# Feed-forward gate and up products turned round: weights stationary, both token halves moving, from the fifth width block on

## The chip, the core and the metric

The kernel runs on one core of a Trainium2 chip. A time is the device time of one execution in microseconds (us); the kernel before was timed three times. TensorE (PE in the profile) multiplies: it holds a 128x128 *stationary* operand, loaded by its own instruction (PEld), and streams a *moving* operand of up to 512 columns through it into a PSUM bank. VectorE (DVE) and ScalarE (ACT) read PSUM and on-chip memory; SyncE (SP) issues the transfers. Each engine works through its own queue in order.

## The reference

Two layers over 256 tokens of width 1024. In each, four token mixers and their gates are summed, projected and added to x, and then comes the part that is changed, a feed-forward block with inner width 2816:

```python
h = rmsnorm(x, g_pre_ffn[l])
f = (jax.nn.silu(h @ w_ffn_gate[l]) * (h @ w_ffn_up[l])) @ w_ffn_down[l]
x = x + rmsnorm(f, g_post_ffn[l])
```

## The kernel before

**Products.** Every operand of a large product is split into two float32r parts, high and low, and a product is made of three passes (`mac`): high x high, low x high, high x low. Tokens lie in two halves of 128. For most products a half's activations (`hh` high, `hl` low, transposed to 128 rows of width by 128 tokens) are stationary, and a weight tile moves.

**Weights.** They come in pieces of 128 x 1024 in the order of use (`PLAN`). `stage` loads a piece into one of four `st` buffers; `convert` (L253, ScalarE) writes its high part; `settle` (L272, VectorE) writes the low part by a subtraction. Both parts lie in `u` slots, of which there are 24, shared with what the attention keeps. `pump` runs ahead of the use as long as slots are free and fewer than six unused pieces lie ready; `tick`, called after every *unit* of the main stream (one piece for one half), calls it, and also moves on the work that runs beside (`spawn`, with a delay counted in ticks). The order of all queues follows from the order in which the program emits; nothing is rearranged later.

**Feed-forward.** The inner width is taken in six blocks (512, 256, 512, 512, 512, 512). For each block and half, gate and up products go into a PSUM bank of 128 tokens x 512. `gate_evict` multiplies with the token's 1/rms (`rf[h]`, one number per partition, since tokens lie on partitions) under the sigmoid, `g_act` multiplies with up, then TensorE transposes the result in blocks of 128x128 (`tp`, L403), and ScalarE and VectorE split it into two `s2k` tiles, the stationary operands of the down products, which run one width block behind. The last two width blocks' down products come at the end of the layer, half 0 first, with the norm (`bank_done`, `g_turn`, `final`).

**The step ahead of it.** The output projection does half 0 first, then half 1. `g_turn` for a half sums squares (ScalarE), takes 1/sqrt by three Newton steps (`rsqrt`, nine small VectorE operations), updates x, transposes it (TensorE), writes `hh` (ScalarE, L483) and `hl` (VectorE, L486), and then by the squares of the new x computes `rf[h]`. Its parts come at fixed tick distances. The first width block starts with seven units of half 0 (`lead_order`), while half 1 is still being turned; before half 1's first unit everything of its `g_turn` that isn't emitted yet is emitted (`finish`).

Of the kernel before, what the change touches and what calls it, by code (L numbers as in the profile page):

```python
# [26 lines left out]
FFW = [512, 256, 512, 512, 512, 512]  # L27
FFO = [0, 512, 768, 1280, 1792, 2304]
# [20 lines left out]
# column groups of w_in: (name, [column ranges])  # L49
# [8 lines left out]
# per-layer tables of small operands (one row per partition): SM large, SG gains and the like  # L58
# [46 lines left out]
def uses(key):  # L105
    """How many units of the program read the piece."""
    return 4 if key[1] in ("uq", "ukv") or key[1:3] == ("fd", len(FFW) - 1) else 2


def kxn(w, k0, nk, cols):  # L110
    """Rows k0*128.. of w (nk blocks of 128) and the columns, as [128, nk * ncols]."""
    parts = [w[k0 * P:(k0 + nk) * P, a:b] for a, b in cols]
    m = np.concatenate(parts, axis=1) if len(parts) > 1 else parts[0]
    n = m.shape[1]
    return m.reshape(nk, P, n).transpose(1, 0, 2).reshape(P, nk * n)


def q_cols(hd):
    """The columns of a head of w_uq: the rope part as it is and with its halves exchanged, beside the rest."""
    o = 96 * hd  # L120
    rp = [(o + 64, o + 96), (o + 80, o + 96), (o + 64, o + 80)]
    return [(o, o + 64)] + rp if hd % 2 == 0 else rp + [(o, o + 64)]


def host_piece(inp, key):
# [16 lines left out]
    if g in ("fg", "fu"):  # L142
        w = FFW[key[2]]
        nk = PIECE // w
        return kxn(inp["w_ffn_gate" if g == "fg" else "w_ffn_up"][l], nk * key[3], nk, [(FFO[key[2]], FFO[key[2]] + w)])
    if g == "fd":
        return kxn(inp["w_ffn_down"][l], FFO[key[2]] // P + key[3], 1, [(0, 1024)])
# [15 lines left out]
def host_const(inp):  # L163
    """Tables that follow from the shapes alone (rope cos and sin, 1/count of the first tokens) and the gains."""
# [22 lines left out]
def trunk(ctx: ExitStack, tc, x, xT, wall, small, const, qtab, gpost, out):  # L187
# [30 lines left out]
    def U(shape, dt=F32):  # L218
        """One of the 4 KB slots that the weights share with what the attention keeps."""
        return T(shape, "u4", NU, dt, wp)  # L220

    def keep(shape):
# [3 lines left out]
        return U(shape)  # L226

# [15 lines left out]
    def cuts(i, w):  # L243
        """The first pieces come in two parts, so that the first products start early."""
# [22 lines left out]
    def settle(keep=0, between=()):  # L267
        """Emit the low parts still owed, all but the last few."""
# [8 lines left out]
    def pump(n=1, between=()):  # L277
        """Load and split up to n pieces, while there is room for them."""
# [24 lines left out]
    def mac(out_, a, aw, w, ws, start, stop):  # L303
        """out += a^T w in three passes; a, w are pairs (hi, lo) of float32r tiles."""
# [58 lines left out]
    def g_rsqrt(res, m, n, m2=None):  # L363
        """res gets 1 / sqrt(m (+ m2) + EPS) for [P, n], by Newton's iteration in steps."""
# [51 lines left out]
    def unit(l, name, i, h, st_, out_, width, nk=2):  # L416
        """Products of half h with piece i of a group (nk blocks of rows), then a step of what runs beside."""
# [6 lines left out]
    def pairs(npc):  # L424
        """The halves in turn, two pieces each."""
# [3 lines left out]
    def lead_order(n):  # L429
        """Units of two halves, half 0 first at the start of a phase."""  # L430
# [3 lines left out]
    def trail_order(n):  # L434
        """Units of two halves, half 0 done early at the end of a phase."""
# [23 lines left out]
    def bank_done(po, n, gp, tn):  # L459
        """The part of a norm that needs one bank: its sum of squares and its product with the gains."""  # L460
# [7 lines left out]
    def g_turn(tn, h, g, hT, rs):  # L468
        """x += rmsnorm * gains for half h, then (x * g)^T in hT[h] and rstd of x in rs[h]."""
# [7 lines left out]
        hh, hl = hT_tiles(h)  # L477
# [19 lines left out]
    def final_start(tn):  # L497
        """EPS and the first bank's part of the mean square, for the last half."""
# [72 lines left out]

    for l in range(NL):
# [7 lines left out]
        def rope(h, dst, src, nh):  # L580
            """dst, src: [P, nh, 32]"""
# [77 lines left out]
        def g_bank(h, b, hp, po):  # L659
            """Scores, softmax and values of the hp heads from b * hp on, for the queries of half h."""  # L660
# [68 lines left out]
        st = {}  # L729

        def g_misc():
# [18 lines left out]
            # convolution  # L750
# [14 lines left out]
            # pooling  # L765
# [29 lines left out]
            # spatial gating  # L795
# [100 lines left out]
        # sigmoid(v) = (1 + tanh(v / 2)) / 2; the last half is taken with the sum  # L896
# [62 lines left out]
        rf = [None, None]  # L959
        hF = [None, None]  # L960
        gturn = [None, None]
        po = [[acc(), acc()] for _ in range(2)]
        tns = [[], []]
        for h, u in trail_order(8):
# [5 lines left out]
            if u == 7:  # L970
                gturn[h] = spawn(g_turn(tns[h], h, sg["gpf"], hF, rf), 0)
# [4 lines left out]
        pd = [None, None]  # L976
        act = {}
        nff = len(FFW)

        def gate_evict(h, pg_, w):  # L980
            sg_ = tok()
            nc.scalar.activation(sg_[:, :w], pg_[:, :w], AF.Sigmoid, scale=rf[h])  # L982
            a = tok()
            nc.vector.scalar_tensor_tensor(a[:, :w], pg_[:, :w], rf[h], sg_[:, :w], op0=ALU.mult, op1=ALU.mult)  # L984
            return a

        def g_act(c, h, pu_, a, w):
            nc.vector.scalar_tensor_tensor(a[:, :w], pu_[:, :w], rf[h], a[:, :w], op0=ALU.mult, op1=ALU.mult)
            yield AY
            t = tp()  # L990
            transposes(t, [a[:, i * P:(i + 1) * P] for i in range(w // P)])
            ah = T([P, 4, P], "s2k", 10, F32R)
            al = T([P, 4, P], "s2k", 10, F32R)
            split_copy(ah.rearrange("p k t -> p (k t)")[:, :w], al.rearrange("p k t -> p (k t)")[:, :w], t[:, :w])
            act[c, h] = (ah, al)

        def down_units(c, h):
            nk = FFW[c] // P
            if c < nff - 1:
                return [(c, h, [i], [0, 1]) for i in range(nk)]  # L1000
            return [(c, h, [i, i + 1], [n]) for n in range(2) for i in range(0, nk, 2)]

        def down(u):
            c, h, ks, ns = u
            for i in ks:
                pc_ = W((l, "fd", c, i))
                for n in ns:
                    mac(pd[h][n], act[c, h], np.s_[:, i, :], pc_, np.s_[:, n * 512:(n + 1) * 512],
                        start=(c == 0 and i == 0), stop=(c == nff - 1 and i == FFW[c] // P - 1))

        gact = {}
        for c, w in enumerate(FFW):
            nkp = PIECE // w
# [98 lines left out]
```

## Time and profile before

| | |
|---|---|
| median of three runs | 809.22 us (808.39 to 810.48) |
| profiled execution, span from first to last instruction | 808.4 us |
| its own time beside the span | no more than the lowest run, 808.39 us |
| TensorE products busy | 797.1 us, 99% |
| TensorE weight loads busy | 662.2 us, 82% |
| VectorE busy | 535.3 us, 66% |
| ScalarE busy | 426.4 us, 53% |
| mean share of the 16 transfer engines | 54% for the weight queue |

In the rows below, a line of the timeline has the start, the duration, the engine, the line of the code, the operation with what it writes and reads, the shape, and how many like it follow one another; in brackets stands the idle time just before and what ended it. A group row has the count, the busy time, the mean in ns, and the idle time. A row of TensorE ends by a model and overlaps the next one, so what one product costs is the distance between starts.

### The profile page before, as it was taken

The numbers are of one execution on the slowest core, as the hardware profiler recorded it, in microseconds if no ns is written. First come the engines' busy times: TensorE is split into PE (matmuls) and PEld (weight loads), VectorE is DVE, ScalarE is ACT, GpSimd is POOL, SyncE is SP. The second block draws the span as 40 slices with busy tenths as digits, with TensorE's granted clock in tenths as the row PEclk, the third lists the DMA queues.
The fourth block names the chain that finished last, engine by engine and source line by source line (L and its number), as shares of the span: only waits on it lengthen the run. The fifth ranks groups of instructions, "written<-read, shape, count | busy, mean of one in ns | idle before, by whom it ended". The sixth has DMA issues, their size and how long they took to land.

```text
span 808.4 us, 10402 instructions
## 1 busy us (share of the span) xinstructions
PE 797.1 (99%) x3857; PEld 662.2 (82%) x3857; DVE 535.3 (66%) x895; ACT 426.4 (53%) x672; POOL 3.9 (0%) x16
## 2 busy tenths in 40 slices
PE   8999999999999999999999999999999999999996
PEld 7878887888789888888888888878888988888885
DVE  5687976657786456554785788765689754554553
ACT  6768655535655335443575686554466534543441
POOL 0000000000000000000000000000000000000000
PEclk9999999999999999999999999999999999999999
DMA  8776454464574555664555645346464574665531
GB/s 272 280 250 207 160 182 145 147 225 160 185 222 159 194 179 171 206 207 155 199 165 183 220 168 183 131 157 206 164 224 160 183 234 156 186 216 154 174 105 52
DMA packets 42226, 148.08 MB, mean 183 GB/s; under 512 B 4672, under 2 KB 5824, under 8 KB 42176
## 3 DMA queue, kind: packets, MB, share of 16 engines
q1 hardware_dynamic: 41600, 145.33, 54.0%
q0 software_dynamic: 576, 2.10, 0.7%
q8 instruction: 30, 0.49, 0.3%
q14 instruction: 20, 0.16, 0.1%
HBM read 146.36 MB, written 1.05 MB: 182 GB/s over the span
## 4 chain that ended last, share of the span: by engine, by line
PE 94%; DMA 3%; DVE 1%; ACT 1%; SPq 0%; issue 0%; DVEq 0%; ACTq 0%
PE acc L305 19%; PE acc L307 19%; PE acc L306 19%; PE mm L307 10%; PE mm L305 10%; PE mm L306 10%; PE tp L403 4%; DMA st<-wall 2%; PE mm L667 1%; DMA x<-x 1%; PE acc L695 1%; DVE u L272 0%; ACT junk L393 0%; ACT u L253 0%; SPq L237 0%
## 5 line engine op out<-in xcount | busy, mean ns | idle before, releaser
L272 DVE TENSOR_TENSOR u<-st,u 128x1024 fp32r<-128x1024 f32 (+2 forms) x272 | 320.0, 1207 | 61.6 <-ACT u L253 61.1
L253 ACT ACTIVATE u<-st 128x1024 fp32r<-128x1024 f32 (+2 forms) x272 | 278.2, 1045 | 76.2 <-DMA st<-wall 72.9
L305 PE MATMUL acc<-u,hh 128*128 128x512 f32 (+1 forms) x464 | 185.9, 401 | 0.8 <-ACT hh L540 0.8
L307 PE MATMUL acc<-u,hh 128*128 128x512 f32 (+1 forms) x464 | 181.0, 390 | 1.0 <-DVE u L272 1.0
L306 PE MATMUL acc<-u,hl 128*128 128x512 f32 (+1 forms) x464 | 180.6, 389 | 0.0
L305 PE MATMUL mm<-u,hh 128*128 128x512 f32 (+1 forms) x368 | 137.3, 373 | 0.0
L307 PE MATMUL mm<-u,hh 128*128 128x512 f32 (+1 forms) x368 | 136.6, 371 | 0.5 <-DVE u L272 0.5
L306 PE MATMUL mm<-u,hl 128*128 128x512 f32 (+1 forms) x368 | 136.4, 371 | 0.0
L307 PEld LDWEIGHTS acc<-u,hh 128*128 128x128 f32 x464 | 87.7, 189 | 19.8 <-DVE u L272 2.2
L305 PE MATMUL acc<-u,s2k 128*128 128x512 f32 x256 | 103.5, 404 | 0.0
L305 PEld LDWEIGHTS acc<-u,hh 128*128 128x128 f32 x464 | 87.8, 189 | 17.7 <-ACT hh L540 1.5
L306 PEld LDWEIGHTS acc<-u,hl 128*128 128x128 f32 x464 | 87.8, 189 | 16.0 <-DVE hl L545 0.3
L307 PE MATMUL acc<-u,s2k 128*128 128x512 f32 x256 | 100.4, 392 | 0.0
L306 PE MATMUL acc<-u,s2k 128*128 128x512 f32 x256 | 100.1, 391 | 0.0
L307 PEld LDWEIGHTS mm<-u,hh 128*128 128x128 f32 x368 | 69.3, 188 | 12.8 <-DVE u L272 0.9
L306 PEld LDWEIGHTS mm<-u,hl 128*128 128x128 f32 x368 | 69.4, 188 | 11.8
L305 PEld LDWEIGHTS mm<-u,hh 128*128 128x128 f32 x368 | 69.3, 188 | 11.7
L307 PEld LDWEIGHTS acc<-u,s2k 128*128 128x128 f32 x256 | 48.1, 188 | 11.0
L950 ACT ACTIVATE gate<-acc,rhalf 128x512 f32<-128x512 f32 x32 | 22.1, 690 | 66.1 <-PE acc L307 66.0
L305 PEld LDWEIGHTS acc<-u,s2k 128*128 128x128 f32 x256 | 48.2, 188 | 9.4 <-issue 0.3
L306 PEld LDWEIGHTS acc<-u,s2k 128*128 128x128 f32 x256 | 48.2, 188 | 9.1
L984 DVE SCALAR_TENSOR_TENSOR tok<-mm,ry,tok 128x512 f32<-128x512 f32 (+1 forms) x22 | 15.4, 700 | 58.8 <-ACT tok L982 58.8
(138 smaller groups left out, 568.0 us busy)
## 6 DMA issues: line engine op xcount, KB each, us to landing
st<-wall SPq DMA_DIRECT2D x261, 512.0 KB, 4.4
st<-wall SPq DMA_DIRECT2D x7, 416.0 KB, 4.1
gpost<-gpost POOLq DMA_DIRECT2D x4, 512.0 KB, 3.8
x<-x SPq DMA_DIRECT2D x1, 1024.0 KB, 7.5
small<-small SPq DMA_DIRECT2D x2, 512.0 KB, 4.2
u<-xT SPq DMA_DIRECT2D x3, 256.0 KB, 8.3
st<-wall SPq DMA_DIRECT2D x2, 256.0 KB, 4.4
out<-x SPq DMA_DIRECT2D x2, 256.0 KB, 2.0
```

The source lines that it names most:

```text
L253: nc.scalar.activation(hi[:, a:b], st[:, a:b], AF.Copy)
L272: nc.vector.tensor_tensor(lo[:, a:b], st[:, a:b], hi.bitcast(F32)[:, a:b], op=ALU.subtract)
L305: nc.tensor.matmul(out_, a[0][aw], w[0][ws], start=start, stop=False)
L306: nc.tensor.matmul(out_, a[1][aw], w[0][ws], start=False, stop=False)
L307: nc.tensor.matmul(out_, a[0][aw], w[1][ws], start=False, stop=stop)
L403: nc.tensor.transpose(dst[:, i * P:(i + 1) * P], s, ident)
L667: nc.tensor.matmul(s3[:, i, :], qT[hd // 4][:, hd % 4, h * P:(h + 1) * P], kT[hd % 2][:, hd // 2, 0:kend], start=True, stop=True)
L695: nc.tensor.matmul(o, v_sb[kb][:, hd, :], pT[:, j * P:(j + 1) * P], start=(kb == 0), stop=(kb == nkb - 1))
L950: nc.scalar.activation(gt[h], pgt[h], AF.Tanh, scale=rhalf[h])
L984: nc.vector.scalar_tensor_tensor(a[:, :w], pg_[:, :w], rf[h], sg_[:, :w], op0=ALU.mult, op1=ALU.mult)
```

## The change

The first width block (512, blocks 0 to 3 of 128) stays as it was. From the fifth block of 128 on, up to the 22nd, gate and up are computed transposed, in blocks of 128 of the inner width: the weight block is stationary and the tokens move. `hx` holds for each of eight row blocks the high parts of both halves and the low parts of both halves side by side (512 columns), in four of the `u` slots, reserved before the output projection and given back after the last gate_up. Per row block, one product with the high weight moves all 512 columns, and one with the low weight moves the 256 high ones. `total` adds the two parts of the bank and multiplies with `rrow`, the 1/rms of the tokens along the free dimension, which `g_rrow` makes by transposing two tiles of copies of `rf`. The result needs no transpose: it is split as it is. Down products run four blocks of 128 behind (`DLAG`), the last eight at the end as before. Pieces of gate and up are now read by one unit each, and `tick` is called in the middle of each product block and again after it.

```diff
-FFW = [512, 256, 512, 512, 512, 512]
-FFO = [0, 512, 768, 1280, 1792, 2304]
+FW = 512
+NB = DFF // P
+B0 = FW // P
+DLAG, DLAST = 4, 8
...
+def down_after(b):
+
+    return [b - DLAG] if b - DLAG < NB - DLAST else []
...
-        for c, w in enumerate(FFW):
-            np_ = 8 * w // PIECE
-            plan += [((l, "fg", c, i), 1024) for i in range(np_)]
-            plan += [((l, "fu", c, i), 1024) for i in range(np_)]
-            if c > 0:
-                plan += [((l, "fd", c - 1, i), 1024) for i in range(FFW[c - 1] // P)]
-        c = len(FFW) - 1
-        plan += [((l, "fd", c, i), 1024) for i in range(FFW[c] // P)]
+        plan += [((l, g, i), 1024) for g in ("fg", "fu") for i in range(8 * FW // PIECE)]
+        for b in range(B0, NB):
+            plan += [((l, "wg", b), 1024), ((l, "wu", b), 1024)]
+            plan += [((l, "fd", i), 1024) for i in down_after(b)]
+        plan += [((l, "fd", i), 1024) for i in range(NB - DLAST, NB)]
...
+        hx = []
+        state["reserve"] += NK // 2
+
+        def hx_parts(h):
+            if not hx:
+                hx[:] = [keep_r([P, 2, 2, SEQ]) for _ in range(NK // 2)]
+            return Part(hx, 0, h), Part(hx, 1, h)
...
-                gturn[h] = spawn(g_turn(tns[h], h, sg["gpf"], hF, rf), 0)
+                gturn[h] = spawn(g_turn(tns[h], h, sg["gpf"], hF, rf, hx_parts), 0)
...
+        rrow = T([P, SEQ], "rrow", 1)
+
+        def g_rrow():
+
+            rb = tok()
+            for h in range(2):
+                nc.vector.tensor_copy(rb[:, h * P:(h + 1) * P], rf[h].to_broadcast([P, P]))
+            yield 1
+            t = tp()
+            transposes(t, [rb[:, h * P:(h + 1) * P] for h in range(2)])
+            nc.scalar.copy(rrow, t[:, :SEQ])
+
+        def block(key):
+
+            pc_ = W((l,) + key)
+            o = mm()
+            for k in range(NK):
+                ws = np.s_[:, k * P:(k + 1) * P]
+                nc.tensor.matmul(o, pc_[0][ws], hx[k // 2][:, k % 2].rearrange("p s t -> p (s t)"),
+                                 start=(k == 0), stop=False)
+                nc.tensor.matmul(o[:, :SEQ], pc_[1][ws], hx[k // 2][:, k % 2, 0, :], start=False, stop=(k == NK - 1))
+                if k == NK // 2 - 1:
+                    tick()
+            return o
+
+        def total(dst, o):
+            nc.scalar.copy(dst, o[:, SEQ:2 * SEQ])
+            nc.vector.tensor_tensor(dst, o[:, 0:SEQ], dst, op=ALU.add)
+            nc.vector.tensor_tensor(dst, dst, rrow, op=ALU.mult)
+
+        def gate_up(b):
+            v, sg_ = tok(), tok()
+            gv, uv = v[:, 0:SEQ], v[:, SEQ:2 * SEQ]
+            total(gv, block(("wg", b)))
+            nc.scalar.activation(sg_[:, :SEQ], gv, AF.Sigmoid)
+            nc.vector.tensor_tensor(gv, gv, sg_[:, :SEQ], op=ALU.mult)
+            tick()
+            total(uv, block(("wu", b)))
+            nc.vector.tensor_tensor(gv, gv, uv, op=ALU.mult)
+            t = T([P, 2, SEQ], "s2k", 10, F32R)
+            split_copy(t[:, 0, :], t[:, 1, :], gv)
+            for h in range(2):
+                act[b, h] = (t[:, 0, h * P:(h + 1) * P], t[:, 1, h * P:(h + 1) * P])
+            tick()
...
+        for h, u in lead_order(8):
+            if u == 0:
+                finish(gturn[h])
+                if h == 1:
+                    rr = spawn(g_rrow(), 1)
...
+        finish(rr)
+        for b in range(B0, NB):
+            gate_up(b)
+            if b == B0:
+                pd = [[acc(), acc()] for _ in range(2)]
+            for i in down_after(b):
+                for h in range(2):
                     if i == 0:
...
+                        finish(gact[h])
+                    down((h, [i], [0, 1]))
                     tick()
...
+        drop(NK // 2)
```

How the queues change is seen at three places. The first is TensorE in the first width block, first layer, between the second and the third unit of half 1. Here `u_418` and `u_428` are weight pieces (`u_421` before), `u_437` and `u_438` are parts of `hx`, and `tok` holds the copies of `rf`. Before:

```order
L306 MATMUL acc_2247<-u_418_1927,hl_470_2165 128x512 [waits DVE_49]
L307 MATMUL acc_2247<-u_419_1928,hh_469_2164 128x512
L305 MATMUL acc_2247<-u_421_1939,hh_469_2164 128x512 [waits Activation_49]
L306 MATMUL acc_2247<-u_421_1939,hl_470_2165 128x512 [waits DVE_49]
L307 MATMUL acc_2247<-u_422_1940,hh_469_2164 128x512
```

Now:

```order
L320 MATMUL acc_2236<-u_419_1928,u_437_2019 128x512
L416 MATMUL tp_2257<-ident_69,tok_2243 128x128 [waits DVE_49] x2
L318 MATMUL acc_2236<-u_428_1985,u_438_2020 128x512 [waits Activation_49]
L319 MATMUL acc_2236<-u_428_1985,u_438_2020 128x512
L320 MATMUL acc_2236<-u_429_1986,u_438_2020 128x512
```

Two transposes that wait for VectorE now stand between the units.

The second place is VectorE while half 1 is turned, same layer: the last `hl`, then `rf` of half 1 (`ms`, `rv`, `ry`, `ra`). Before:

```order
L486 SCALAR_TENSOR_TENSOR hl_470_2165<-tp_2192,cst_74,hh_469_2164 128x128 x3
L272 TENSOR_TENSOR u_474_2183<-st_2125,u_473_2182 128x1024 [waits DMAHW1_49]
L272 TENSOR_TENSOR u_479_2209<-st_2137,u_478_2208 128x1024 [waits DMAHW2_49,Activation_49]
L372 SCALAR_TENSOR_TENSOR rv_2234<-ms_2217 128x1 [waits Activation_49]
L373 TENSOR_SCALAR ry_2235<-rv_2234 128x1 [waits DVE_49]
L374 TENSOR_SCALAR rv_2234<-rv_2234 128x1 [waits DVE_49]
L272 TENSOR_TENSOR u_485_2226<-st_2149,u_484_2225 128x1024 [waits DMAHW3_49,PE_49,Activation_49]
L378 SCALAR_TENSOR_TENSOR ra_2236<-ry_2235,rv_2234 128x1 [waits DVE_49]
```

Now:

```order
L499 SCALAR_TENSOR_TENSOR u_439_2021<-tp_2193,cst_74,u_439_2021 128x128 x2
L285 TENSOR_TENSOR u_475_2184<-st_2128,u_474_2183 128x1024 [waits DMAHW1_49,PE_49]
L385 SCALAR_TENSOR_TENSOR rv_2224<-ms_2213 128x1 [waits Activation_49]
L386 TENSOR_SCALAR ry_2225<-rv_2224 128x1 [waits DVE_49]
L387 TENSOR_SCALAR rv_2224<-rv_2224 128x1 [waits DVE_49]
L391 SCALAR_TENSOR_TENSOR ra_2226<-ry_2225,rv_2224 128x1 [waits DVE_49]
...
L395 SCALAR_TENSOR_TENSOR ry_2225<-ra_2226,ry_2225 128x1 [waits DVE_49]
L1034 COPY tok_2243<-ry_2084 128x128
L1034 COPY tok_2243<-ry_2225 128x128 [waits DVE_49]
```

One weight subtraction instead of two stands ahead of the steps and none among them, and the two copies for `rrow` close them.

The third place is ScalarE in the output projection, where half 0's two banks are squared (`junk`). Before:

```order
L253 ACTIVATE u_418_1927<-st_1882 128x1024 [waits DMAHW1_49,DVE_49]
L253 ACTIVATE u_421_1939<-st_1894 128x1024 [waits DMAHW2_49,DVE_49]
L393 ACTIVATE junk_1950,ms_1948<-acc_1865 128x512 [waits PE_49]
L253 ACTIVATE u_427_1962<-st_1913 128x1024 [waits DMAHW3_49,DVE_49]
L393 ACTIVATE junk_1971,ms_1948<-acc_1866 128x512 [waits PE_49,Activation_49]
```

Now:

```order
L266 ACTIVATE u_418_1927<-st_1882 128x1024 [waits DMAHW1_49,DVE_49]
L406 ACTIVATE junk_1945,ms_1943<-acc_1865 128x512 [waits PE_49]
L406 ACTIVATE junk_1960,ms_1943<-acc_1866 128x512 [waits PE_49,Activation_49]
L266 ACTIVATE u_428_1985<-st_1894 128x1024 [waits DMAHW2_49,DVE_49]
L266 ACTIVATE u_431_1997<-st_1913 128x1024 [waits DMAHW3_49,DVE_49]
```

Two conversions have moved behind the second square.

More of the change, by code (lines that the diff above doesn't have):

```diff
@@ L226, in keep, with keep_r @@
         return U(shape)
+    def keep_r(shape):
+        state["free"] -= 1
+        state["reserve"] -= 1
+        assert state["free"] >= 0 and state["reserve"] >= 0
+        return U(shape, F32R)
     def drop(n):
@@ L985, in gate_evict, with g_act @@
             return a
-        def g_act(c, h, pu_, a, w):
-            nc.vector.scalar_tensor_tensor(a[:, :w], pu_[:, :w], rf[h], a[:, :w], op0=ALU.mult, op1=ALU.mult)
+        def g_act(h, pu_, a):
+            nc.vector.scalar_tensor_tensor(a[:, :FW], pu_, rf[h], a[:, :FW], op0=ALU.mult, op1=ALU.mult)
             yield AY
             t = tp()
-            transposes(t, [a[:, i * P:(i + 1) * P] for i in range(w // P)])
+            transposes(t, [a[:, i * P:(i + 1) * P] for i in range(B0)])
@@ L992, in g_act @@
             ah = T([P, 4, P], "s2k", 10, F32R)
             al = T([P, 4, P], "s2k", 10, F32R)
[L994 to L1001, printed above, removed]
+            split_copy(ah.rearrange("p k t -> p (k t)"), al.rearrange("p k t -> p (k t)"), t)
@@ new lines, in g_act @@
+            for i in range(B0):
+                act[i, h] = (ah[:, i, :], al[:, i, :])
+        rrow = T([P, SEQ], "rrow", 1)
[18 more added lines that the diff above has]
+            return o
@@ L1003, in down, with down_units @@
+        def down_units(h):
+            i = NB - DLAST
+            return [(h, [b], [0, 1]) for b in range(i, NB - 4)] + \
+                   [(h, [b, b + 1], [n]) for n in range(2) for b in range(NB - 4, NB, 2)]
         def down(u):
-            c, h, ks, ns = u
-            for i in ks:
-                pc_ = W((l, "fd", c, i))
+            h, bs, ns = u
+            for b in bs:
+                pc_ = W((l, "fd", b))
                 for n in ns:
-                    mac(pd[h][n], act[c, h], np.s_[:, i, :], pc_, np.s_[:, n * 512:(n + 1) * 512],
-                        start=(c == 0 and i == 0), stop=(c == nff - 1 and i == FFW[c] // P - 1))
@@ new lines, in down @@
+                    mac(pd[h][n], act[b, h], np.s_[:, :], pc_, np.s_[:, n * 512:(n + 1) * 512],
+                        start=(b == 0), stop=(b == NB - 1))
+        gact = [None, None]
+        pb, a = {}, {}
+        for h, u in lead_order(8):
[3 more added lines that the diff above has]
+                    rr = spawn(g_rrow(), 1)
+            g, i = u // 4, u % 4
+            if i == 0:
+                pb[h, g] = mm() if h == 0 else acc()
+            unit(l, (("fg", "fu")[g],), i, h, hF, pb[h, g], FW)
+            if i == 3:
+                if g == 0:
+                    a[h] = gate_evict(h, pb[h, 0])
+                else:
+                    gact[h] = spawn(g_act(h, pb[h, 1], a[h]), 0)
+            tick()
@@ L1053, in trunk @@
         hT, rstd = [None, None], [None, None]
-        us = [down_units(nff - 2, h) + down_units(nff - 1, h) for h in range(2)]
+        us = [down_units(h) for h in range(2)]
         tns = [[], []]
```

74 lines of the change are left out of this document (23 added, 51 removed).

## The prediction

> **What bounds the kernel now.** I read the page first: busy shares, then the chain of waits.
>
> ```profile
> PE 797.1 (99%) x3857; PEld 662.2 (82%) x3857; DVE 535.3 (66%) x895; ACT 426.4 (53%) x672; POOL 3.9 (0%) x16
> PE 94%; DMA 3%; DVE 1%; ACT 1%; SPq 0%; issue 0%; DVEq 0%; ACTq 0%
> ```
>
> TensorE is busy 99% of the span and is 94% of the chain that ended last. So the change is worth what it takes from or adds to TensorE's own row of work, and whatever makes TensorE wait. The span is 808.4 us, equal to the lowest run (808.39) within the rounding, so nothing lies around it; the median of the three runs is 809.22, 0.8 above. I sum against 808.4 and add 0.8 at the end.
>
> A busy TensorE row lasts longer than its share of the queue, so prices come from the spacing of starts in the timeline. First the 512-column products and a group of four transposes, then the products of 256 columns, then the weight loads under them (a group row):
>
> ```profile
> 258.03 0.38 PE L403 MATMUL tp<-ident,tok 128*128 128x128 f32 x2
> 258.48 0.39 PE L306 MATMUL acc<-u,s2k 128*128 128x512 f32 x1
> ...
> 318.10 0.60 PE L403 MATMUL tp<-ident,tok 128*128 128x128 f32 x4
> 318.78 0.40 PE L306 MATMUL acc<-u,s2k 128*128 128x512 f32 x1
> 319.01 0.39 PE L307 MATMUL acc<-u,s2k 128*128 128x512 f32 x1
> 321.07 0.40 PE L307 MATMUL acc<-u,s2k 128*128 128x512 f32 x1
> 327.26 0.39 PE L305 MATMUL mm<-u,hh 128*128 128x512 f32 x1
> 344.50 0.39 PE L306 MATMUL mm<-u,hl 128*128 128x512 f32 x1
> ```
>
> ```profile
> 65.49 0.28 PE L305 MATMUL mm<-s2k,u 128*128 128x256 f32 x1
> 66.76 0.28 PE L307 MATMUL mm<-s2k,u 128*128 128x256 f32 x1
> 244.12 0.28 PE L305 MATMUL mm<-u,hh 128*128 128x256 f32 x1
> 247.60 0.28 PE L307 MATMUL mm<-u,hh 128*128 128x256 f32 x1
> ```
>
> ```profile
> L307 PEld LDWEIGHTS mm<-u,hh 128*128 128x128 f32 x368 | 69.3, 188 | 12.8 <-DVE u L272 0.9
> ```
>
> 512 columns: 76 starts from 327.26 to 344.50 make 0.2268 us each (gate and up), 9 from 319.01 to 321.07 make 0.2289 (down). 256 columns: 29 from 244.12 to 247.60 make 0.120, 11 from 65.49 to 66.76 (weights stationary) make 0.1155. The weight loads take 0.188 each and still the products start every 0.120, so the loads are hidden even at 256 columns.
>
> **Part 1: transposes of the results go.** From 318.10 to 318.78 stand four transposes and one product: 0.68 - 0.229 = 0.45. A pair (258.03 to 258.48) costs 0.45 - 0.229 = 0.22. Per layer four wide blocks lose 8 groups of four, the narrow one 2 pairs: 8 x 0.45 + 2 x 0.22 = 4.05, in two layers **-8.1**. The new rrow adds a pair per layer: **+0.4**.
>
> **Part 2: the products.** For one 128-wide block and one of the 8 row blocks the old wide form spends 1.5 products of 512 columns (six over four blocks): 0.340. The narrow form spends three of 256: 0.360. The new form is one of 512 and one of 256: 0.2268 + 0.120 = 0.347; low end 0.2268 + 0.1155 = 0.342, high end 0.2289 + 0.120 = 0.349. Per layer that is 16 x 2 x 8 = 256 such pairs from wide blocks and 32 from the narrow one. Low: 512 x 0.002 - 64 x 0.018 = 0. High: 512 x 0.009 - 64 x 0.011 = +3.9. I take **+2.0**, the middle: the weights are stationary as in the 0.1155 row, but the moving tile is a u slot held like those of the 0.120 row.
>
> The columns streamed are the same; what grows is the number of weight loads, by 576 - 480 = 96 a layer. [...]
>
> **Part 3: rrow makes TensorE wait.** The two transposes of rrow stand in TensorE's queue after nine units of the first block (seven of half 0, two of half 1), and their input needs rstd of half 1, a chain of ScalarE squares, nine tiny VectorE steps and two copies. Before, that rstd was needed only by gate_evict, on other engines. Rows of the first layer, then of the second, then an undisturbed run of the nine steps, then the nearest row for a broadcast copy:
>
> ```profile
> 218.84 0.39 PE L305 MATMUL mm<-u,hh 128*128 128x512 f32 x1
> 232.01 0.39 PE L305 MATMUL acc<-u,hh 128*128 128x512 f32 x1
> ...
> 230.15 1.12 DVE L486 SCALAR_TENSOR_TENSOR hl<-tp,cst,hh 128x128 fp32r<-128x128 f32 x4
> 231.19 2.35 DVE L272 TENSOR_TENSOR u<-st,u 128x1024 fp32r<-128x1024 f32 x2
> ...
> 232.06 0.18 ACT L393 ACTIVATION_READ_ACCUMULATOR junk<-x 128x1 f32 x1
> ...
> 627.84 0.39 PE L305 MATMUL acc<-u,hh 128*128 128x512 f32 x1
> ...
> 627.01 2.35 DVE L272 TENSOR_TENSOR u<-st,u 128x1024 fp32r<-128x1024 f32 x2
> ...
> 397.35 0.15 DVE L372 SCALAR_TENSOR_TENSOR rv<-ms 128x1 f32<-128x1 f32 x1
> 399.06 0.16 DVE L382 SCALAR_TENSOR_TENSOR ry<-ra,ry 128x1 f32<-128x1 f32 x1
> L602 DVE COPY kr<-kr 128x96 f32<-128x96 f32 x4 | 1.0, 253 | 0.1
> ```
>
> TensorE enters the block at 218.84 and would issue the pair at 232.01. In VectorE's new order one 1024-wide subtraction (not two) stands between the last hl and the nine steps: 231.19 + 1.13 = 232.3. ScalarE's squares are done by 232.24 even in the old order, with a conversion ahead that is now gone. Nine steps: 399.22 - 397.35 = 1.9. Two copies, the second starting behind the first: about 0.5. So rrow's input is there at 234.7, 2.7 us after TensorE asked. Second layer: 627.01 + 1.13 + 1.9 + 0.5 = 630.5 against 627.84, again 2.7. Together **+5.4**. Low end, if the subtraction falls behind the steps: 2 x 1.6 = 3.2; high end, if another stands ahead: 2 x 3.8 = 7.6. Queued behind the waiting pair are the rest of half 1's products, so nothing of it is hidden: TensorE has no slack to give back.
>
> **Part 4: a stall in the first layer goes.** Reserving four slots for hx before the output projection takes weight conversions out of ScalarE's queue there (the order rows above).
>
> ```profile
> 207.39 1.06 ACT L253 ACTIVATE u<-st 128x1024 fp32r<-128x1024 f32 x1 [2.77 <-DMA st<-wall]
> 208.36 0.58 ACT L393 ACTIVATE junk<-acc 128x512 f32<-128x512 f32 x1
> ...
> 211.58 1.42 DVE L474 SCALAR_TENSOR_TENSOR x<-mrg,ry,x 128x512 f32<-128x512 f32 x2
> ...
> 211.13 0.39 PE L307 MATMUL acc<-u,hh 128*128 128x512 f32 x1
> 212.43 0.63 PE L403 MATMUL tp<-ident,x 128*128 128x128 f32 x4 [0.91 <-PE acc L307]
> ```
>
> TensorE waits 0.91 for x, late because the square of the second bank sat behind a conversion that a transfer delayed to 207.39. Without it in front the square can start when the bank is done. The transposes follow after four more units (24 products x 0.227 = 5.4 us before 211.36, at 205.9), x comes two microseconds sooner and the wait goes: **-0.9**, between 0 and -1.0.
>
> **Part 5: VectorE and ScalarE get more, smaller work.** Per block VectorE now does seven operations of 256 columns and ScalarE four, where four blocks together had six and four of 512.
>
> ```profile
> L407 DVE TENSOR_TENSOR s2k<-tp,s2k 128x256 fp32r<-128x256 f32 x4 | 1.7, 426 | 4.1 <-ACT s2k L406 4.0
> L982 ACT ACTIVATE tok<-mm,ry 128x256 f32<-128x256 f32 x4 | 1.9, 475 | 5.6 <-PE mm L307 5.5
> L406 ACT ACTIVATE s2k<-tp 128x256 fp32r<-128x256 f32 x4 | 1.5, 386 | 6.5 <-PE tp L403 6.5
> ```
>
> In its fixed order, a block's VectorE work is: five operations whose successor waits for them at 0.46 (0.426 and a short hand-over), two at 0.35 (overlapped by the next), the sigmoid (0.475) and the split copy (0.386) waited for with some 0.03 each, and weight subtractions at 1.13: 2.3 + 0.7 + 0.95 = 3.95 plus 1.13 each. With three subtractions that is 7.35 of a TensorE period of 16 x 0.347 + 12 x 0.229 = 8.3: covered. In the last four blocks of a layer, without down products, it is 3.95 + 2.26 = 6.2 against 5.55: VectorE falls behind by 0.65 a block, 2.6 in four. A PSUM bank is needed again 2.8 us after its block ends and is freed by ScalarE's copy and VectorE's addition some 1.0 after it, so 1.8 is slack; and the last two down pieces have their low parts ready about when used. I take 0.5 per layer, **+1.0**; low end 0, high end 2 x 2.6 = +5.
>
> **Sum.** -8.1 + 0.4 + 2.0 + 5.4 - 0.9 + 1.0 = -0.2: span 808.2, with the 0.8 of the median 809.0. The gain of the transposes is spent on the wait for rrow.
>
> **The rivals.**
>
> Rival A, the wait for rrow doesn't come (rstd of half 1 earlier than I place it, or the pair later). For it: only queue order, not time, is known of the new code. Against it: the pair's place and its input are fixed by the order, and the input chain is read from rows of both layers. Time: 809.0 - 5.4 = 803.6. Chance 0.15.
>
> Rival B, VectorE becomes the bound in the last four blocks: if the seven short operations and two hand-overs cost 0.1 more each, a block takes 7.1 against 5.55, 6.2 behind after four, less 1.8 slack: 4.4 per layer against the 0.5 taken, +7.8: 816.8; half of that extra gives 813. It decides from 0.45 us a block of excess on (1.8 over four). Against it: in whole blocks with down products VectorE keeps 0.9 us, so it enters the stretch caught up. Chance 0.13.
>
> Rival C, the clock. At the kernel's start products of 416 columns start every 0.35 and a few microseconds later every 0.19, although the granted clock reads 1.00 throughout:
>
> ```profile
> 9.20 0.55 PE L306 MATMUL acc<-u,hl 128*128 128x416 f32 x1
> 9.55 0.55 PE L307 MATMUL acc<-u,hh 128*128 128x416 f32 x1
> 14.42 0.35 PE L306 MATMUL acc<-u,hl 128*128 128x416 f32 x1
> 14.61 0.35 PE L307 MATMUL acc<-u,hh 128*128 128x416 f32 x1
> ```
>
> So the array does have a half-speed start. If a wait of 2.7 us put it back there for some five microseconds, each layer would lose 2.5: 809.0 + 5 = 814. Against it: after the 0.91 wait the full spacing was back at once; none of 2.7 is in this trace. [...] Chance 0.07.
>
> **How the numbers follow.** The sum's own case (wait for rrow, products between their ends) has 0.65, spread about 806 to 812. A has 0.15, B 0.13, C 0.07. What this kernel's measurement can tell from no change is about 0.3%, 2.4 us: 806.8 to 811.6. Faster: A and the low end of the sum (products at 0.342, a shorter wait), 0.15 + 0.12 = 0.27. Slower: B, C and the high end, 0.20 + 0.04 = 0.24. Within: 0.49. The range 803.4 to 813 takes in A and part of B and C; the likeliest case's own is 806 to 812.
>
> **What would show it.** In the changed profile the transposes of tok fall by 72 and rise by 4, and TensorE rows number about 3857 + 192 - 68 = 3981. Part 1 and 2: pairs of a 512 and a 256 product start every 0.342 to 0.349, and the stretch from one block's first product to the next is 8.3 us. Part 3: an idle of about 2.7 us before two transposes with releaser DVE, once a layer, some 13 us after the first feed-forward product. Part 4: no wait of the first four x transposes. Part 5: VectorE waits little in the last four blocks of a layer, and TensorE waits for an addition on mm or for the last u there, under 1 us in all. I am wrong if the pair's spacing is outside its ends, if the wait is under 1.5 or over 4 us, or if VectorE already trails in the blocks with down products.

## The result and the profile after

The changed kernel takes 819.95 us, the median of five runs (817.64 to 821.76), beside 809.47 us for the kernel before (five runs, 808.39 to 810.48). The ratio is 1.0129, 95% interval 1.0114 to 1.0145: 10.5 us slower. The prediction was 809.0 with a range to 813.0.

The profiled execution has a span of 819.3 us, 10.9 more than before. Its device time is 821.12: wherever both are known, the device time is 1.7 to 1.8 us above the span. So the span of 808.4 before belongs to an execution of some 810.1 us (an estimate from this difference), and not to the lowest run, 808.39, to which the table ahead of the prediction sets it equal. The page's busy shares and its chain of waits first, then the table of TensorE's waits (releaser, us in total, times, longest):

```profile
PE 800.7 (98%) x3981; PEld 667.3 (81%) x3981; DVE 598.6 (73%) x1091; ACT 452.8 (55%) x778; POOL 3.9 (0%) x16
PE 81%; DVE 10%; ACT 4%; DMA 3%; issue 1%; SPq 0%; DVEq 0%; ACTq 0%
```

```profile
PE tp L416 <- DVE tok L1034: 4.4, 2, 2.2
PE acc L318 <- ACT s2k L419: 1.9, 2, 1.0
PE acc L320 <- DVE u L285: 1.5, 5, 0.4
PE mm L363 <- POOL ident masks.py:199: 1.4, 1, 1.4
PE tp L416 <- DVE x L487: 1.3, 1, 1.3
PE acc L318 <- ACT hh L553: 0.9, 1, 0.9
PE acc L319 <- DVE s2k L420: 0.5, 2, 0.2
```

TensorE's share of the chain fell from 94% to 81%, and VectorE's rose from 1% to 10%. Three waits are new: rrow's transposes (the first row), the activations of the first width block (the second and the last), and x between the layers (the fifth). Two more costs do not stand in this table, and they are of like size.

**The clock behind the wait for rrow.** TensorE's rows around that wait in the first layer, then busy times by stretch (engines in the order PE, PEld, DVE, ACT, POOL, then the granted TensorE clock, the share of the DMA engines and GB/s):

```profile
230.14 0.39 PE L320 MATMUL acc<-u,u 128*128 128x512 f32 x1
232.73 0.69 PE L416 MATMUL tp<-ident,tok 128*128 128x128 f32 x2 [2.20 <-DVE tok L1034]
233.07 0.78 PE L318 MATMUL acc<-u,u 128*128 128x512 f32 x1
233.64 0.63 PE L319 MATMUL acc<-u,u 128*128 128x512 f32 x1
...
235.78 0.53 PE L318 MATMUL acc<-u,u 128*128 128x512 f32 x1
236.14 0.39 PE L319 MATMUL acc<-u,u 128*128 128x512 f32 x1
```

```profile
226.00:230.30 4.30, 4.30 (x20) 3.39 (x19) 4.15 (x11) 4.27 (x12) 0.00 (x0) 1.00 0.79 245
230.50:232.70 2.20, 0.03 (x1) 0.00 (x0) 1.92 (x12) 0.09 (x1) 0.00 (x0) 0.98 0.77 259
232.70:236.10 3.40, 3.37 (x9) 2.79 (x10) 2.47 (x3) 1.84 (x3) 0.00 (x0) 0.51 0.52 177
```

The pair is 2.36 us late (2.59 from start to start, less one product of 0.229). Behind it products start every 0.43 us instead of 0.227, and the granted clock reads 0.51 for 3.4 us. These slow products cost 1.46 us over their normal spacing here and 1.66 in the second layer.

**The price of a pair.** The end of the second transposed block (block 5), and the down product behind them:

```profile
260.27 0.28 PE L1048 MATMUL mm<-u,u 128*128 128x256 f32 x1
260.39 0.40 PE L1046 MATMUL mm<-u,u 128*128 128x512 f32 x1
260.62 0.28 PE L1048 MATMUL mm<-u,u 128*128 128x256 f32 x1
260.74 0.39 PE L318 MATMUL acc<-u,s2k 128*128 128x512 f32 x1
```

The pair from 260.39 takes 0.35. Over all 576 of them a start follows a 512-column product by 0.236 and a 256-column one by 0.117 on average: 0.353. A block with its down products takes 8.41 us. The old form needed 33.68 us for four such blocks (first down products at 315.35 and at 349.03), 8.42 each, so in the steady stretch the change gains next to nothing.

The two feed-forward stages account for the difference. From the first feed-forward product to the next layer's first product the time was 187.75 us (218.84 to 406.59) and is 194.19 (217.19 to 411.38), +6.4. In the second layer, up to the last product, it was 186.51 and is 192.65, +6.1. Between the two stages (208.07 and 208.06) and behind the last product (7.2 both times) nothing changed. Ahead of the first stage TensorE is 1.65 earlier. Of that, 1.17 come behind TensorE's 201st row (at 51.11 before, at 50.63 now), where the wait of 0.91 for x is gone. The rest is the start of the kernel, which differs between executions: the changed kernel and its variants, with the same program on TensorE up to there, reach the stage at 216.2 to 218.7. Where single executions are compared below, the lengths of the two stages are the surer measure.

### The profile page after: what moved, and what is told of

Read it like the earlier page. It is cut to its first block, busy times and chain, and to the rows that moved or that the text cites. A ratio compares the mean times of both kernels' runs of the same rounds, so it can differ in the third digit from the quotient of the medians.

```text
span 819.3 us, 10893 instructions
## 1 busy us (share of the span) xinstructions
PE 800.7 (98%) x3981; PEld 667.3 (81%) x3981; DVE 598.6 (73%) x1091; ACT 452.8 (55%) x778; POOL 3.9 (0%) x16
## 4 chain that ended last, share of the span: by engine, by line
PE 81%; DVE 10%; ACT 4%; DMA 3%; issue 1%; SPq 0%; DVEq 0%; ACTq 0%
PE acc L320 18%; PE acc L318 18%; PE acc L319 18%; PE mm L1046 13%; PE mm L1048 6%; DVE u L285 4%; DMA st<-wall 3%; PE tp L416 3%; PE mm L690 1%; DVE tok L1056 1%; DVE tok L1055 1%; PE acc L718 1%; PE mm L318 1%; PE mm L320 1%; PE mm L319 1%
## 5 line engine op out<-in xcount | busy, mean ns | idle before, releaser
L1046 PE MATMUL mm<-u,u 128*128 128x512 f32 x576 | 204.7, 398 | 0.0
L318 PE MATMUL acc<-u,hh 128*128 128x512 f32 (+1 forms) x432 | 173.4, 401 | 0.9 <-ACT hh L553 0.9
L320 PE MATMUL acc<-u,hh 128*128 128x512 f32 (+1 forms) x432 | 168.6, 390 | 1.1 <-DVE u L285 1.1
L319 PE MATMUL acc<-u,hl 128*128 128x512 f32 (+1 forms) x432 | 168.4, 390 | 0.0
L1048 PE MATMUL mm<-u,u 128*128 128x256 f32 x576 | 161.8, 281 | 0.0
L1046 PEld LDWEIGHTS mm<-u,u 128*128 128x128 f32 x576 | 108.2, 188 | 26.4
L1048 PEld LDWEIGHTS mm<-u,u 128*128 128x128 f32 x576 | 108.8, 189 | 1.2
L320 PEld LDWEIGHTS acc<-u,hh 128*128 128x128 f32 x432 | 81.8, 189 | 18.8 <-DVE u L285 2.3
L318 PEld LDWEIGHTS acc<-u,hh 128*128 128x128 f32 x432 | 81.8, 189 | 16.3 <-ACT hh L553 1.4
L319 PEld LDWEIGHTS acc<-u,hl 128*128 128x128 f32 x432 | 81.9, 190 | 14.7 <-DVE hl L558 0.3
L1055 DVE TENSOR_TENSOR tok<-mm,tok 128x256 f32<-128x256 f32 x72 | 30.2, 420 | 34.6 <-ACT tok L1054 34.6
L1054 ACT COPY tok<-mm 128x256 f32<-128x256 f32 x72 | 26.6, 369 | 51.2 <-PE mm L1048 47.0
L419 ACT ACTIVATE s2k<-tok 128x256 fp32r<-128x256 f32 (+1 forms) x38 | 16.3, 429 | 52.5 <-DVE tok L1066 52.5
```

The lines of the kernel that those rows point to most:

```text
L318: nc.tensor.matmul(out_, a[0][aw], w[0][ws], start=start, stop=False)
L319: nc.tensor.matmul(out_, a[1][aw], w[0][ws], start=False, stop=False)
L320: nc.tensor.matmul(out_, a[0][aw], w[1][ws], start=False, stop=stop)
L419: nc.scalar.activation(hi, src, AF.Copy)
L1046: nc.tensor.matmul(o, pc_[0][ws], hx[k // 2][:, k % 2].rearrange("p s t -> p (s t)"), start=(k == 0), stop=False)
L1048: nc.tensor.matmul(o[:, :SEQ], pc_[1][ws], hx[k // 2][:, k % 2, 0, :], start=False, stop=(k == NK - 1))
```

## The experiments

TensorE's share of each cost could be read from the profile, but not what brings it about. The theory from the profile: the wait for rrow, a clock that falls in the wait, a dearer pair, a first down product that now comes too early, and a VectorE that trails at the layers' ends. Rivals were put beside each in the expectations. The first four runs shared a chip with runs of the kernel before at 810.47 us (median), the next four at 809.79, the last two at 810.53. The changed kernel lay 10.3 us above the kernel before in the last comparison, so I set savings against 820.8 on the first chip and 820.1 on the second.

### rrow's transposes later

```diff
-            yield 1
+            yield 4
             t = tp()
             transposes(t, [rb[...] for h in range(2)])
```

> Only the two transposes of rrow stand three units (4.1 us) later in TensorE's queue; VectorE's order is the same. Theory: the 2.2 us wait in each layer goes, and with it the stretch behind it in which eight products start every 0.43 us, since the idle time brought that about: 2 x 2.36 + 1.46 + 1.66 = 7.8 us less, 812.1. Rival: the slow stretch belongs to the place (parts of hx being written, weights landing) and stays: 4.7 less, 815.2, and products at 0.43 are still seen there.

Measured: 814.51 us, ratio 1.0059 (1.0047 to 1.0071), 6.3 less than the change. In TensorE's table of waits the row of rrow is gone:

```profile
PE acc L318 <- ACT s2k L419: 1.9, 2, 1.0
...
PE tp L416 <- DVE x L487: 1.0, 1, 1.0
```

No product in that place starts at 0.43 any more. 6.3 lies between the two expectations: the waits alone are 4.7, and 1.6 is left for the slow stretch, about half of the 3.1 that the profiled execution showed. Between the two profiled executions the theory's 7.8 is met: the feed-forward stages take 189.98 and 188.93 for 194.19 and 192.65, 7.9 less.

### The wait filled with work

```diff
             t = tp()
+            for k in range(12):
+                nc.tensor.matmul(t, hx[0][:, 0, 0, 0:P],
+                                 hx[0][:, k % 2].rearrange("p s t -> p (s t)"), start=True, stop=True)
             transposes(t, [rb[...] for h in range(2)])
```

> Twelve products of 512 columns, whose result is thrown away, stand ahead of the transposes of rrow, so that TensorE is busy for 2.7 us while rrow's input is made. Theory: the time of the wait stays spent (2.7 in place of 2.36 a layer, +0.7), but nothing runs at 0.43 behind it, -3.1: 817.5. Rival (the slow stretch has nothing to do with the idle time): 820.7, with the products behind the transposes still at 0.43.

Measured: 819.34 us, ratio 1.0113 (1.0100 to 1.0126), 1.5 less than the change although TensorE does 24 products more. The stretch behind the first of them, by granted clock:

```profile
231.20:234.60 3.40, 3.40 (x18) 2.79 (x17) 3.12 (x13) 0.48 (x3) 0.00 (x0) 1.00 0.65 246
632.60:636.00 3.40, 3.40 (x17) 2.80 (x16) 3.08 (x13) 0.49 (x2) 0.00 (x0) 1.00 0.73 245
```

The clock stays at 1.00 in both layers. The same place, with the same operands and transfers, is not slow when TensorE has no idle time ahead of it. Four places without a slow stretch, in two executions, could still be chance; the next runs settle it. The filled place costs 0.7 more than the wait in the two layers (2 x 2.72 against 2 x 2.36, both over the normal spacing), as expected, so the slow stretch was worth about 2.2 in these runs.

### A shorter and a longer wait, and the change again

The transposes one unit later (`yield 2`); rrow's copies made six times over (`for h in 6 * [0, 1]`); and the changed kernel once more.

First the shorter wait:

> The transposes of rrow stand one unit (1.36 us) later, so about 0.85 us of each wait is left. In the runs so far a wait of 2.2 us was followed by products every 0.43 four times in six. Theory: a wait as short as 0.85 us leaves the array at full speed: 820 - 2 x 1.36 - 2.1 = 815, and no product behind the waits at 0.43. Rival: any wait can bring the slow stretch: 817, products at 0.43 seen in one layer or both.

Then the longer one:

> rrow's two copies are made six times over on VectorE, one behind the other, so that TensorE's wait grows from 2.2 to about 4.2 us a layer; nothing else changes. In the profiles so far a 2.2 us wait was followed by the slow stretch four times in eight. Theory: the longer the idle time, the surer the fall (an activity window that runs on its own, so that it matters how much of the idle time falls into one): slow products behind the wait in both layers, 820 + 2 x 2.0 + 3.1 x 0.5 = 825.5. Rival: the fall is a matter of chance whatever the length: 824, slow in one layer of two or none.

And the change:

> The changed kernel itself once more beside the longer wait. 820, and with its two waits of 2.2 us two more looks at whether the slow stretch follows: one of two by the count so far.

Measured: 815.87 us (ratio 1.0089, 1.0065 to 1.0113), 825.26 us (1.0181, 1.0160 to 1.0202), and 820.83 us (1.0139, 1.0112 to 1.0165). The shorter wait comes out nearer its theory's 815 than the rival's 817, and the clock behind it stays at 1.00 in both layers; for the longer one the two expectations lie too near each other for the time to decide, so the clock does. The change again, behind its first wait, then the longer wait and what follows it in both layers:

```profile
231.60:233.90 2.30, 0.16 (x1) 0.00 (x0) 2.02 (x12) 0.22 (x1) 0.00 (x0) 1.00 0.74 242
233.90:237.30 3.40, 3.34 (x16) 2.80 (x17) 2.50 (x4) 2.36 (x4) 0.00 (x0) 1.00 0.60 176
```

```profile
230.70:234.30 3.60, 0.09 (x1) 0.00 (x0) 3.32 (x22) 0.15 (x1) 0.00 (x0) 1.00 0.72 245
234.30:237.80 3.50, 3.45 (x9) 2.81 (x10) 2.49 (x3) 1.91 (x3) 0.00 (x0) 0.51 0.35 91
634.50:638.10 3.60, 0.13 (x1) 0.00 (x0) 3.32 (x22) 0.18 (x1) 0.00 (x0) 0.86 0.66 248
638.10:643.80 5.70, 5.61 (x15) 4.46 (x16) 2.53 (x4) 2.38 (x3) 0.00 (x0) 0.50 0.51 152
```

The same program with the same wait of 2.2 us shows no slow stretch in this execution, in either layer. Counted over all profiles that have it (the change twice, and the grouped, the later-down and the unscaled kernels below), a wait of 2.2 us was followed by the half clock 4 times in 10. The wait of 0.84 us was followed by it 0 times in 2, the longer one (3.56) 2 times in 2. The other stalls from 20 us on, 0.91 to 1.52 us each and over twenty, never were.

The traces also show what goes with the fall. In each of these executions the granted clock changed only in steps of 3.413 us: in the change its two falls, at 232.63 and 635.40, lie 402.77 apart, 118 steps, and each time it stayed at half for one step (for two, 6.83 us from 637.11, in the longer wait's second layer). No run shows what sets the steps. The table has the idle time that fell into one of them. Where a wait brought no fall, the steps are continued from the clock's other changes in that execution, at the kernel's start and end.

| kernel | first layer: most idle time in one step, clock in the next | second layer |
|---|---|---|
| the change | 2.10 us, half | 2.19 us, half |
| the change again | 1.72 us, full | 1.73 us, full |
| products grouped | 1.94 us, half | 1.79 us, full |
| down products later | 1.32 us, full | 2.21 us, half |
| up product unscaled | 1.46 us, full | 1.34 us, full |
| shorter wait | 0.84 us, full | 0.84 us, full |
| longer wait | 3.41 us, half | 2.48 us, half |

Here are the step with the wait and the step behind it in the grouped kernel, first layer and then second:

```profile
231.19:234.61 3.42, 1.48 (x8) 1.26 (x9) 2.88 (x12) 0.97 (x2) 0.00 (x0) 1.00 0.62 201
234.61:238.02 3.41, 3.41 (x10) 2.67 (x9) 1.23 (x1) 1.52 (x3) 0.00 (x0) 0.50 0.67 207
630.55:633.97 3.42, 1.63 (x8) 1.01 (x6) 3.17 (x12) 1.68 (x3) 0.00 (x0) 1.00 0.77 214
633.97:637.38 3.41, 2.99 (x14) 2.54 (x15) 2.73 (x6) 2.28 (x3) 0.00 (x0) 1.00 0.63 189
```

So the idle time within one step parts the cases, as the longer wait's theory had it: behind 1.94 us and more the clock read half in 6 of 6, behind 1.79 and less in 0 of 8. Waits of 2.2 us differ in how they lie on the steps: 1.34 to 2.21 us of them fell into one. At the kernel's start the half clock also came behind steps with 1.82 us (the change again) and 1.75 us (the filled wait) of idle time, whose longest waits are 1.52 and 1.35, at 15.02 and 14.92.

The longer wait came out at 3.6, not the 4.2 expected, and added 4.4 us to the time: 2.7 of wait, and the rest fits the clock.

### Products of a kind together

```diff
+            ws = [np.s_[:, k * P:(k + 1) * P] for k in range(NK)]
             for k in range(NK):
-                ws = np.s_[:, k * P:(k + 1) * P]
-                nc.tensor.matmul(o, pc_[0][ws], ...)
+                nc.tensor.matmul(o, pc_[0][ws[k]], ...)
-                nc.tensor.matmul(o[:, :SEQ], pc_[1][ws], hx[k // 2][:, k % 2, 0, :], ...)
-                if k == NK // 2 - 1:
+                if k == 5:
                     tick()
+            for k in range(NK):
+                nc.tensor.matmul(o[:, :SEQ], pc_[1][ws[k]], hx[k // 2][:, k % 2, 0, :], ...)
```

The `tick` in the block's middle moves to the sixth wide product, which is about the same time into the block (1.37 us for 1.41).

> In each gate and up block the eight products of 512 columns come first and then the eight of 256, in place of taking turns. Theory: taking turns costs, and like after like gives the spacing of the rows of before, 0.2268 + 0.1155 = 0.342 for 0.353: 576 x 0.011 = 6.3 us less, 813.6. Rival: the price belongs to each product (its weight load, its start) whatever stands beside it: no change, 820, a block of 16 pairs still takes 5.65.

Measured: 817.88 us, ratio 1.0095 (1.0082 to 1.0109), 2.9 less than the change, between the two. One block in the timeline (eight products to a row):

```profile
255.63 1.99 PE L1046 MATMUL mm<-u,u 128*128 128x512 f32 x8
257.46 1.12 PE L1051 MATMUL mm<-u,u 128*128 128x256 f32 x8
258.41 2.00 PE L1046 MATMUL mm<-u,u 128*128 128x512 f32 x8
...
261.21 0.39 PE L318 MATMUL acc<-u,s2k 128*128 128x512 f32 x1
```

Eight products of 512 take 1.83 (0.229 each), eight of 256 take 0.95 (0.119): 0.348 a pair for 0.353. A block with its down products takes 8.33 instead of 8.41, and 36 x 0.08 = 2.9 is the whole gain. So taking turns costs 0.005 a pair. The rest over my 0.347 is that 512 columns in this form take 0.229, the spacing of the down products, and not the 0.2268 of the old gate and up products. What makes that difference isn't settled by these runs.

### Down products one block later

```diff
-DLAG, DLAST = 4, 8
+DLAG, DLAST = 5, 8
-    return [b - DLAG] if b - DLAG < NB - DLAST else []
+    return [b - DLAG] if 0 <= b - DLAG < NB - DLAST else []
```

> Down products run five blocks behind in place of four, so that the first of them comes after block 5, and three blocks at a layer's end in place of four have none. Theory: the 1.7 us stall in the first down product of each layer goes, because the split of half 1, which stands on ScalarE behind block 4's split, is done by then: -3.4, 816.6; with VectorE trailing over three blocks for four, up to 1.5 more, 815. Rival: half 1's activations are late of themselves or ScalarE's order moves with the down products: the stall is seen again one block later, 820.

Measured: 815.39 us, ratio 1.0067 (1.0055 to 1.0079), 5.4 less than the change. First the stall as the change has it: VectorE, ScalarE and TensorE while the first down products run, then TensorE's waits with the later down products.

```profile
251.69 0.42 DVE L1066 TENSOR_TENSOR tok<-tok 128x256 f32<-128x256 f32 x1
...
253.09 0.69 DVE L420 TENSOR_TENSOR s2k<-tp,s2k 128x512 fp32r<-128x512 f32 x1
...
252.15 0.42 ACT L419 ACTIVATE s2k<-tok 128x256 fp32r<-128x256 f32 x1 [1.42 <-DVE tok L1066]
252.47 0.58 ACT L419 ACTIVATE s2k<-tp 128x512 fp32r<-128x512 f32 x1
...
253.11 0.49 PE L318 MATMUL acc<-u,s2k 128*128 128x512 f32 x1 [0.95 <-ACT s2k L419]
253.83 0.50 PE L319 MATMUL acc<-u,s2k 128*128 128x512 f32 x1 [0.23 <-DVE s2k L420]
```

```profile
PE tp L416 <- DVE tok L1034: 4.4, 2, 2.2
...
PE tp L416 <- DVE x L487: 0.3, 1, 0.3
```

Half 1 of the first width block is transposed at 250.16, and its copy from the bank (ScalarE, 252.47) could start soon after. But on ScalarE it stands behind block 4's copy (252.15), which waits 1.42 for block 4's chain of three operations on VectorE. TensorE, at half 1's first down product, waits for both parts: 1.12 + 0.49 + 0.11 over the normal spacing, 1.72 us per layer. With the down products one block later both rows of s2k are gone, and the wait for x has shrunk from 1.28 to 0.28. The theory holds on both points.

### Less work for VectorE

```diff
-        def total(dst, o):
+        def total(dst, o, r=True):
...
-            nc.vector.tensor_tensor(dst, dst, rrow, op=ALU.mult)
+            if r:
+                nc.vector.tensor_tensor(dst, dst, rrow, op=ALU.mult)
...
-            total(uv, block(("wu", b)))
+            total(uv, block(("wu", b)), False)
-            nc.vector.scalar_tensor_tensor(a[:, :FW], pu_, rf[h], a[:, :FW], op0=ALU.mult, op1=ALU.mult)
+            nc.vector.tensor_tensor(a[:, :FW], pu_, a[:, :FW], op=ALU.mult)
```

> The up product is not multiplied by the tokens' 1/rms (neither in the first width block nor after it; the norm behind the down product takes that factor out again, but for its epsilon), so VectorE has one 256-column operation (0.45 us) less per block. Theory: VectorE needs 5.7 us per block in the last four of a layer in place of 6.15, TensorE 5.65, so it no longer trails: the wait for x between the layers (1.45) and those for the last low parts of the weights (0.74) nearly go, and the first down product waits 0.45 less in each layer: 820 - 2.0 - 0.9 = 817. Rival: the wait for x comes from the transfers of the next layer's weights alone and stays: 819.

Measured: 815.09 us, ratio 1.0073 (1.0053 to 1.0093), 5.0 less than the change. First the end of the first layer in the change, ScalarE's and VectorE's rows; TensorE is done with the gate and up products at 386.97. Then TensorE's waits with the lighter VectorE.

```profile
390.53 0.42 ACT L419 ACTIVATE s2k<-tok 128x256 fp32r<-128x256 f32 x1 [1.67 <-DVE tok L1066]
395.69 0.90 ACT L266 ACTIVATE u<-st 128x832 fp32r<-128x832 f32 x1 [2.06 <-DMA st<-wall]
...
400.42 0.57 ACT L406 ACTIVATE junk<-acc 128x512 f32<-128x512 f32 x1
...
391.32 4.42 DVE L285 TENSOR_TENSOR u<-st,u 128x1024 fp32r<-128x1024 f32 x4
404.11 1.41 DVE L487 SCALAR_TENSOR_TENSOR x<-mrg,ry,x 128x512 f32<-128x512 f32 x2
```

```profile
PE tp L416 <- DVE tok L1034: 4.4, 2, 2.2
...
PE acc L318 <- ACT s2k L419: 1.0, 2, 0.5
PE acc L320 <- DVE u L285: 0.9, 3, 0.4
```

In the change the last copy of a gate and up block comes 3.56 us after TensorE's last product of it, because VectorE trails. Four subtractions follow in one go (391.32), which free the buffers for the next layer's weights; the transfers into them come late, and the square of the second bank (400.42) stands on ScalarE behind conversions that wait for them. With the lighter VectorE that last copy comes 1.73 us behind TensorE and the square 1.7 us earlier, counted from the end of the gate and up products. The conversions still wait for transfers (1.79, 1.21, 0.53), but x is there in time: its row is gone, and so are the waits for the last low parts. The wait of the first down product halves, as expected. The rival falls. That the time fell by 5.0 and not by 3 is not VectorE's doing alone: against the change again, which shows no slow stretch either, the two feed-forward stages got 3.2 shorter (190.69 and 189.61 for 192.53 and 190.95), as forecast. The rest between these two executions, 1.75, lies ahead of the first stage (216.67 for 218.42), where the program on TensorE is the same.

### The edits together

rrow later, products grouped, down products later; then the same with the up product unscaled.

> The three edits together: rrow three units later, products of a kind together, down products five blocks behind. Theory: they work at different places and add up: 820 - 6.4 - 3.0 - 5.5 = 805, under the kernel before. Rival: with the waits gone transfers or VectorE fill the gaps, and a third of it is lost: 810.

> The three edits and the up product left unscaled. Theory: VectorE is no longer the last anywhere, and the stalls that are left at the layers' ends (0.4 and 0.3 in the run with the later down products) go: 804. Rival: nothing waits for VectorE any more with the down products later: as with the three edits alone.

Measured: 806.90 us, ratio 0.9966 (0.9955 to 0.9977), and 804.86 us, ratio 0.9943 (0.9927 to 0.9959). Both are faster than the kernel before, by 2.9 and 4.9 us. The three savings sum to 6.3 + 2.9 + 5.4 = 14.6, and together they gave 13.2, so a tenth of them is lost and not the rival's third. TensorE's waits with the three edits:

```profile
PE acc L318 <- ACT hh L553: 1.8, 2, 0.9
PE mm L363 <- POOL ident masks.py:199: 1.4, 1, 1.4
PE tp L416 <- DVE x L487: 0.6, 1, 0.6
...
```

The first two rows are the kernel's start; what is left in the feed-forward stages is the 0.6 for x and 0.2 for a last low part. With the up product unscaled too, no row of TensorE's table of waits lies in these stages any more, and they take 185.66 and 184.54 us for 186.50 and 185.15 with the three edits and 187.75 and 186.51 before. So the theory for the last run holds, with 1.45 of its 2.0 us seen in the stages; the two spans (803.1 and 803.2) hide it, since the one execution reaches the first stage 1.35 us later than the other. The transposed form does bring a gain, and the change as it was made spent it, and 10 us more, on dearer pairs, the wait for rrow and the clock behind it, the first down products and a trailing VectorE.

## Why the prediction was wrong, step by step

- **What bounds the kernel:** right. Everything that changed the time changed TensorE's row of products or made it wait. That nothing lies around the span was misread (it is 1.7 to 1.8 us), but the forecast adds a difference to a median, so this moved nothing.
- **Part 1, transposes (-8.1, +0.4):** right in number. The transposes of `tok` went from 168 to 100, TensorE's rows to 3981, as forecast.
- **Part 2, the pair (+2.0, ends 0 and +3.9):** mis-sized, and outside its ends. A pair took 0.353 us, not 0.347: 512 x 0.013 - 64 x 0.007 = +6.2. Both ends came from streams of like products, and no row of before had two lengths taking turns. Grouping shows 0.005 of it to be the turns; the rest is 0.229 for 512 columns, which stood among my rows (the down products) as the high end. The 192 loads added last 0.188 us each in the changed kernel's profile too (L1046), 36 us if none were hidden (an estimate from that row). The whole part measured 6.2, so the loads stay hidden here but for at most that.
- **Part 3, the wait for rrow (+5.4):** the mechanism and the place were right, 2.36 us late in each layer for 2.7: +4.7. With the transposes three units later it is gone.
- **Rival C, the clock, which I gave 0.07:** it came true inside the likeliest case: behind the 2.20 us wait the granted clock reads 0.51. I priced it at 5 us; the profiled execution lost 3.1 by it, and the runs on average about 2 (1.6 and 2.2 by the first two experiments). The sum had nothing for it. My argument against it, that the 0.91 us wait had left the clock alone, was a row too short to speak for 2.7. In the runs 1.94 us of idle time within one step of 3.413 us was enough, and the same wait of 2.2 us brought the fall or not.
- **Part 4, the stall for x in the first layer (-0.9):** right. Those transposes start at 210.80 without a wait, and the way to the first stage got 1.2 shorter.
- **Part 5, VectorE (+1.0):** its pace was right, 6.14 to 6.20 us a block against 6.2 forecast (TensorE takes 5.65), but the place was wrong. No bank was late. The lag (3.56 us at the first layer's end) went through the weight buffers to the transfers, to ScalarE's queue and so to x (1.45), and to the last low parts in the second layer (0.74): +2.2. Rival B, at 0.13 and +4 to +7.8, was the same lag at another place and too dear.
- **The step that is missing:** the first down products. Before, 12.4 us lay between the end of the first width block (241.54) and the first down product (253.91); now 6.45 (244.07 to 250.52), since one block of 128 stands there for one of 256. I costed the first block as unchanged and never asked what is late next when the cover behind it is halved: +3.4.

With these sizes the forecast span of 808.2 becomes 808.2 + 4.2 (pair) - 0.7 (wait) + 3.1 (clock) + 3.4 (first down products) + 1.2 (VectorE) = 819.4, against 819.3 in the profiled execution. That they agree to 0.1 is partly luck: in the two feed-forward stages the sizes give 11.9 of the 12.5 measured, and the other way 0.75 come from the earlier start of the first stage. The miss is a price (4.2), the clock (3.1) and waits (3.9), all on one side.

## What to carry to other kernels

When a change shortens the work between a producer and its first consumer, price the new distance against the chain that must fit in it, on every engine's queue in order: here a copy of 0.58 us on ScalarE was late because the one ahead of it had waited 1.42, and TensorE lost 1.72 us a layer by it. A wait of 2.2 us on a busy TensorE was followed by the half clock in 4 of 10 cases, which cost 1.46 and 1.66 us more in the profiled execution of the change; moving the waiting instruction three units down the queue took both away. And where a form of work never occurs in the profile, such as products of two lengths taking turns, its price may lie outside the prices of its parts (here 0.353 us a pair for 0.342 to 0.349), so the range has to be wider than those.

## What the hardware showed unexpectedly

TensorE's granted clock changed only in steps of 3.413 us in these traces. At the waits for rrow it fell to half for the next step (once for two) when 1.94 us or more of a step had been idle (6 of 6 cases), and not at 1.79 or less (0 of 8). The fall can be seen inside a wait: the row from 634.50 to 638.10 reads 0.86, since the clock fell at 637.11. It can also come behind one: in the grouped kernel TensorE was at work again from 233.13 on, and the clock fell at 234.61. By contrast, at the kernel's start, where products of 416 columns are 0.35 apart until about 9.9 us, the granted clock reads 1.00; the trace before holds no value of the clock ahead of 9.97, so the column says nothing there. And products of 512 and 256 columns that take turns cost 0.005 us a pair more than the same products in runs of eight.
